# Projecting q and k of the differential branch first and v last, in a two-layer mixed-branch encoder

## Chip, cores and metric

One core of one Trainium2 chip. The time is in device microseconds for one run of the whole program, the median of several runs. TensorE (PE) does the matmuls and its weight loads show as PEld; VectorE is DVE, ScalarE is ACT, GpSimd is POOL, and SyncE (SP) issues the DMAs.

## The reference

Two layers over two groups of tokens, 512 and 256 of them, with a model width of 1024. Each layer normalises its input, projects it to fourteen pieces with one matrix, runs four branches (latent attention, differential attention, a recurrent gate unit, grouped-query attention), multiplies each by a SiLU gate, and projects the concatenation out.

```python
def diff_branch(q, k, v, pos, lam, subln, layer_idx):
    q = partial_rope(q.reshape(b, s, 2 * H_B, DK_B), pos).reshape(b, s, H_B, 2, DK_B)
    k = partial_rope(k.reshape(b, s, 2 * H_B, DK_B), pos).reshape(b, s, H_B, 2, DK_B)
    v = v.reshape(b, s, H_B, DV_B)
    ...
    o1 = blocked_attention(q[..., 0, :], k[..., 0, :], v, DK_B ** -0.5)
    o2 = blocked_attention(q[..., 1, :], k[..., 1, :], v, DK_B ** -0.5)
    o = o1 - lam_full.astype(o1.dtype) * o2
    o = rms_norm(o, subln) * (1.0 - lam_init)

def rglru_branch(xc, conv_w, conv_b, wa, ba, wx, bx, lam):
    # xconv: a convolution of four taps over xc
    def direction(d, reverse):
        r = jax.nn.sigmoid(blockdiag(xconv, wa[d]) + ba[d]).astype(jnp.float32)
        i = jax.nn.sigmoid(blockdiag(xconv, wx[d]) + bx[d])
        log_a = -LRU_C * r * jax.nn.softplus(-lam[d].astype(jnp.float32))
        a = jnp.exp(log_a)
        gx = jnp.sqrt(-jnp.expm1(2.0 * log_a)) * (i * xconv).astype(jnp.float32)
        _, h = lax.associative_scan(scan_combine, (a, gx), axis=1, reverse=reverse)
        return h
    h = direction(0, False) + direction(1, True)
```

## The kernel before

The 768 tokens are six tiles of 128, four of the first group and two of the second. A float32 product is three matmuls of halves: each operand is split into a high and a low part (`split_evac`, L460: ACT writes the high part at L114, DVE the low one; for weights L211), and `mm3` (L285) runs low by high, high by low and high by high. Inside a layer the program text has this order: grouped-query attention, latent attention, then the stretch that the change touches, then the differential attention with the gates and the next layer's preparation woven in, then the output projection.

The stretch in question holds two generators. `rglru()` makes two tiles of features, ct 0 and 1. For each: a projection with the features on the partitions (24 matmuls of 128x512 and 24 of 128x256), the convolution on DVE (L969 and L972), a copy of its high part on ACT and of its low part on POOL (L980), four gate products a group (the tiles `tr`, by the weights in `pt`), tanh and exp on ACT, a multiplication chain on DVE (L993 to L996), a square root on ACT, and then on DVE L1006, two scans (L1007, L1008) and L1009. `diff()` projects v, q and k in chunks of 256 columns, one token tile after another: 24 matmuls of 128x256 a tile into `acc` or `tr` banks in turn (`ROT_B`). A tile of v is evacuated by two pairs of ACT and DVE (`v_evac`) into tiles of tag `b`; a tile of q or k by a copy on DVE (L193) to a tile of tag `rot` and three short DVE operations that rotate its first columns (L735, L737, L740).

The attention then transposes half of q and k on PE (L622), splits them on ACT and DVE into `b` tiles, and stacks pieces of them by SBUF-to-SBUF DMAs on SyncE: `stacks` issues six a head and score pair (L750 and L752), 24 for a half of the heads. A score product (L764) needs the six of its pair.

The order in which each engine runs is not the program's: `arrange` (from L1267) takes all instructions and issues them again by a list. At each step it takes, over all engines, the instruction that could start soonest by its own cost figures, and of equals the earlier in the program. Buffers of one tag are given out in the order in which the program first writes to them; an instruction that opens a buffer out of its turn has to wait for those before it:

```python
            x = need[tag] = need.get(tag, 0) + 1
            if queue[tag][x - 1:x] != [t] or len(free[tag]) < x:
                return None
            t0 = max(t0, sorted(free[tag])[x - 1])
```

There are 51 buffers of `b`, 6 of `wh` and of `wl` (split weights and loads of the adaptive-norm weights), 2 of `rot`, and 2 `acc`, 3 `tr` and 2 `s` PSUM banks. So the program's order does two things: it breaks ties, and it fixes the order of the buffers. A tile of v opens its pair of `b` buffers when its first half is written, one pair of pairs for two token tiles.

Of the kernel before, what the change touches and what calls it, by code (L numbers as in the profile page):

```python
# [18 lines left out]
P = 128  # L19
# [54 lines left out]
def body(ctx, tc, I, O, dbg=None):  # L74
# [8 lines left out]
    def sb(shape, dt=F32, tag=None, bufs=None):  # L83
        cnt[0] += 1
        nm = f"{tag or 'c'}_{cnt[0]}"
        tag = tag or nm
        return pool.tile(list(shape), dt, name=nm, tag=tag, bufs=bufs or BUFS.get(tag, 1))
# [299 lines left out]
    for l in range(DEPTH):  # L387
# [40 lines left out]
        def token_chunk(ci, evac, loaded=None):  # L428
            ncol = TCH[ci][1]
            his, los = loaded or token_load(ci)  # L430
            for tt in range(NT):
                acc = ps("acc")
                g = 0 if tt < 4 else 1
                s = slice(tt * P - GRP[g][0], (tt + 1) * P - GRP[g][0])
                hh, hl = H[g]
                for k in range(KC):
                    mm3(acc[:, :ncol], hh[k][:, s], hl[k][:, s], his[k // 2][:, k % 2], los[k // 2][:, k % 2],
                        k == 0, k == KC - 1)
                evac(tt, acc)
                yield  # L440
# [86 lines left out]
        def transpose_pv(Ps, g, vt, done):  # L527

            t0, n = GRP[g]
            nk = n // P  # L530
            pv = ps("pv")
            for kt in range(nk):
                tr = ps("tr")
                for qt in range(nk):
                    nc.tensor.transpose(tr[:, qt * P:(qt + 1) * P], Ps[qt // 2][:, qt % 2, kt * P:(kt + 1) * P], ident)  # L535
                ph, pl = (sb([P, 512], F32R, tag="pt") for _ in range(2))
                split_evac(ph[:, :n], pl[:, :n], tr[:, :n])
                for i, p in enumerate((pl, ph)):
                    nc.tensor.matmul(pv[:, :n], vt(g, kt), p[:, :n], start=(kt == 0 and i == 0),  # L539
                                     stop=(kt == nk - 1 and i == 1))  # L540
                if kt % 2:
                    yield
            done(pv)
# [58 lines left out]
        def v_tiles(nh):  # L602

            both = [[sb([P, 2, 2, 2, 64], F32R, tag="b") for _ in range(NT // 2)] for _ in range(nh // 2)]

            def head(h):
                def at(g, kt):
                    tt = GTILES[g][kt]
                    return both[h // 2][tt // 2][:, tt % 2, h % 2].rearrange("p e d -> p (e d)")
                return at  # L610
            return both, [head(h) for h in range(nh)]
# [104 lines left out]
            jobs["d"] = attn  # L716


        def diff():
            both, Vs = v_tiles(4)  # L720

            def evac_v(tt, acc):
                v_evac(both, tt, acc)
            yield from token_chunk(2, evac_v)
            qr = sb([P, NT, 256], tag="rot")
            kr = sb([P, NT, 256], tag="rot")

# [27 lines left out]
            def job(g, cp, half, j, o, dens, after):  # L755
                n = GRP[g][1]
                st = {}

                def soft():
                    st["P"] = []  # L760
                    for h2 in range(n // 256):

                        (p1, d1), (p2, d2) = [softmax(
                            lambda out, qt: nc.tensor.matmul(out, q[:96, qt * P:(qt + 1) * P], k[:96], start=True,  # L764
                                                             stop=True), g, h2, d) for (q, k), d in
                            zip(st["qk"], (dens[:, 2 * h2:2 * h2 + 2, 2 * half + j], None))]
                        V.reciprocal(d2, d2)  # L767
                        V.scalar_tensor_tensor(d2, d2, nlam, d1, op0=ALU.mult, op1=ALU.mult)
                        for i in range(2):
                            V.scalar_tensor_tensor(p1[:, i], p2[:, i], d2[:, i:i + 1], p1[:, i],  # L770
                                                   op0=ALU.mult, op1=ALU.add)
                        st["P"].append(p1)
                        yield

                def pv():
                    yield from transpose_pv(st["P"], g, Vs[2 * half + j], lambda pv: o_evac(o, j, pv, n))
                    after()
                return {"stacks": lambda: st.__setitem__("qk", [stacks(cp(), 2 * j + i, g) for i in range(2)]),
                        "soft": soft, "pv": pv, "w": n // 256}
# [263 lines left out]
        def take(gen, n=10 ** 6):  # L1043
            for _ in range(n):
                if next(gen, 0) == 0:
                    break
# [14 lines left out]
                    due -= 1  # L1061
                    next(fill, None)

        lru, gq = rglru(), gqa()
        rot_acc[:] = ROT_A
        take(gq)
        rot_acc[:] = ["acc"]
# [29 lines left out]
        take(lru, 2)  # L1097
        take(df, 6)
        take(lru, 2)
        take(df, 6)  # L1100
        take(lru)
        take(df)
        rot_acc[:] = ["acc"]
        xsrc = I["x"] if l == 0 else xd
        xs = [[None, None] for _ in range(NT)]
# [161 lines left out]
def arrange(tc):  # L1267
# [59 lines left out]
    group.pop("open", None)  # L1327
    follow = {}
    for k, g in sorted(group.items()):
        deps[g] |= {j for j in deps[k] if j != g and group.get(j) != g}  # L1330
        follow.setdefault(g, []).append(k)
    after = [[] for _ in range(n)]
    todo = [len(d) for d in deps]
# [223 lines left out]
```

## Time and profile before

| what | us |
|---|---|
| median of 3 runs | 943.17 |
| lowest and highest | 938.64, 943.53 |
| the profiled execution | 942.88 |
| its span in the trace | 941.1 |
| PE busy | 866.7 |
| DVE busy | 718.0 |
| ACT busy | 558.4 |
| POOL busy | 150.1 |

The profiled execution is the one that the trace records; its span is from the first to the last instruction, and 1.8 us of the run lie outside it. Busy times are sums over the span, and the engines work at the same time. A row of a timeline gives the start, the duration and the work of an instruction, and in brackets how long its engine had nothing to do before it and what released it. A row "x3" holds three in a row. The end of a matmul is modelled; its pace is read from the starts.

### The profile page before, as it was taken

How to read it: one execution, taken by the hardware profiler on the slowest of the kernel's cores; microseconds unless marked ns; L12 is line 12 of the kernel's file. 1: busy time of each engine (PE TensorE's matmuls, PEld its weight loads, DVE VectorE, ACT ScalarE, POOL GpSimd, SP SyncE). 2: the span in 40 equal slices, each digit the busy share in tenths (PEclk: the TensorE clock that was granted, in tenths of full speed). 3: DMA queues.
4: the chain of work that ended last, by engine and by line, in shares of the span. 5: the costliest groups of instructions: out<-in, count | busy, mean ns of one | idle time of the engine just before them, and what ended most of it. 6: DMA issues, size and time to landing. Idle time of an engine off the chain costs nothing. (4 is left out here: it accounts for less than half of the span.)

```text
span 941.1 us, 15540 instructions
## 1 busy us (share of the span) xinstructions
PE 866.7 (92%) x5248; PEld 723.3 (77%) x5248; DVE 718.0 (76%) x1894; ACT 558.4 (59%) x1355; POOL 150.1 (16%) x168
## 2 busy tenths in 40 slices
PE   4899887999989899899999998799999999998996
PEld 1599676878989675677889976677798887886785
DVE  5677997778498678868556998789756887999645
ACT  5544896777545456645456368688637535777422
POOL 0321011003111010203302201000121222011510
PEclk9999999999999999999999999899999999998998
DMA  9821020313202575227711211021231225324412
GB/s 351 274 74 57 1 68 26 102 59 96 56 24 84 161 229 159 84 63 235 231 49 35 65 37 67 3 68 56 80 102 41 60 70 133 86 67 156 152 46 90
DMA packets 54351, 91.72 MB, mean 97 GB/s; under 512 B 9072, under 2 KB 13936, under 8 KB 54272
## 3 DMA queue, kind: packets, MB, share of 16 engines
q1 hardware_dynamic: 54272, 90.73, 31.3%
q8 instruction: 42, 0.69, 0.3%
q14 instruction: 37, 0.30, 0.1%
HBM read 73.38 MB, written 6.31 MB: 85 GB/s over the span
## 5 line engine op out<-in xcount | busy, mean ns | idle before, releaser
L285 PE MATMUL acc<-wh,b 128*128 128x256 f32 (+4 forms) x720 | 186.6, 309 | 0.0
L285 PE MATMUL acc<-b,wh 128*128 128x512 f32 (+1 forms) x576 | 169.5, 361 | 0.0
L114 ACT ACTIVATE p<-s,mx 128x512 f32<-128x512 f32 (+1 forms) x192 | 117.9, 616 | 39.7 <-DVE mx L520 33.9
L211 POOL TENSOR_TENSOR wl<-ws,wh 128x512 fp32r<-128x512 f32 (+3 forms) x56 | 75.7, 1354 | 368.6 <-ACT wh L114 325.1
L285 PEld LDWEIGHTS acc<-wh,b 128*128 128x128 f32 (+1 forms) x720 | 131.0, 190 | 3.6
L285 PEld LDWEIGHTS acc<-b,wh 128*128 128x128 f32 x576 | 104.8, 191 | 21.4 <-issue 8.0
L285 PE MATMUL acc<-wl,b 128*128 128x256 f32 (+4 forms) x360 | 109.3, 314 | 5.3 <-ACT pt L114 1.6
L285 PE MATMUL tr<-wh,b 128*128 128x256 f32 (+2 forms) x432 | 110.6, 290 | 0.0
L285 PE MATMUL acc<-b,wl 128*128 128x512 f32 (+1 forms) x288 | 102.9, 362 | 1.0 <-DVE den L767 0.5
L520 DVE TENSOR_REDUCE mx<-s 128x1 f32<-128x512 f32 x128 | 86.4, 682 | 12.7 <-PE s L764 9.1
L539 PE MATMUL pv<-pt,b 128*128 128x512 f32 (+1 forms) x288 | 93.5, 392 | 2.6 <-DVE pt L460 2.0
L535 PE MATMUL tr<-c,p 128*128 128x128 f32 x480 | 84.3, 283 | 11.6 <-DVE pt L460 7.5
L460 DVE TENSOR_TENSOR pt<-tr,pt 128x512 fp32r<-128x512 f32 (+1 forms) x144 | 84.5, 594 | 7.7 <-ACT pt L114 6.5
L114 ACT ACTIVATE wh<-ws 128x512 fp32r<-128x512 f32 (+3 forms) x100 | 62.8, 641 | 42.6 <-PE tr L285 12.8
L535 PEld LDWEIGHTS tr<-c,p 128*128 128x128 f32 x480 | 60.9, 145 | 31.1 <-DVE pt L460 9.7
L114 ACT ACTIVATE pt<-tr 128x512 fp32r<-128x512 f32 (+1 forms) x144 | 74.3, 527 | 10.4 <-PE tr L535 9.7
L285 PEld LDWEIGHTS tr<-wh,b 128*128 128x128 f32 x432 | 79.4, 190 | 0.7
L285 PEld LDWEIGHTS acc<-wl,b 128*128 128x128 f32 (+1 forms) x360 | 67.7, 191 | 10.4 <-ACT pt L114 2.2
L285 PEld LDWEIGHTS acc<-b,wl 128*128 128x128 f32 x288 | 54.6, 191 | 14.2 <-issue 8.1
L114 ACT ACTIVATE b<-tr 128x128 fp32r<-128x128 f32 (+7 forms) x92 | 40.0, 448 | 38.3 <-PE tr L285 14.3
L539 PEld LDWEIGHTS pv<-pt,b 128*128 128x128 f32 x288 | 52.3, 200 | 12.6 <-DVE pt L460 6.0
L285 PE MATMUL tr<-wl,b 128*128 128x256 f32 (+2 forms) x216 | 61.1, 290 | 0.0
(254 smaller groups left out, 1905.5 us busy)
## 6 DMA issues: line engine op xcount, KB each, us to landing
ws<-wf SPq DMA_DIRECT2D x40, 256.0 KB, 2.9
b<-ada SPq DMA_DIRECT2D x32, 256.0 KB, 5.4
ws<-wt SPq DMA_DIRECT2D x32, 256.0 KB, 3.3
wl<-ada SPq DMA_DIRECT2D x32, 256.0 KB, 5.2
wh<-ada SPq DMA_DIRECT2D x32, 256.0 KB, 4.5
ws<-wo SPq DMA_DIRECT2D x32, 256.0 KB, 3.2
b<-b SPq DMA_DIRECT2D x112, 64.0 KB, 2.7
b<-b SPq DMA_DIRECT2D x112, 32.0 KB, 1.8
```

The costliest lines, as they stand in the source:

```text
L114: return nc.scalar.activation(out, in_, f, **kw)
L211: engine(eng).tensor_tensor(lo, w, hi.bitcast(F32), op=ALU.subtract)
L285: nc.tensor.matmul(out, s, m, start=first and i == 0, stop=last and i == 2)
L460: V.tensor_tensor(lo, src, hi.bitcast(F32), op=ALU.subtract)
L520: V.tensor_reduce(mx[:, i:i + 1], views[i], axis=AX.X, op=ALU.min)
L535: nc.tensor.transpose(tr[:, qt * P:(qt + 1) * P], Ps[qt // 2][:, qt % 2, kt * P:(kt + 1) * P], ident)
L539: nc.tensor.matmul(pv[:, :n], vt(g, kt), p[:, :n], start=(kt == 0 and i == 0), stop=(kt == nk - 1 and i == 1))
```

## The change

`diff()` is cut in two: v's chunk is a generator of its own, `diff_v()`, and the projections are called in another order. Before: two steps of the recurrent branch (its first feature tile), v, two steps (its second), q, the rest of the branch, then k. After: two steps, q, two steps, k (and the setting up of the attention's jobs), the rest of the branch, then v. An edit in `arrange` writes the sets of dependencies of a group of matmuls in another way, with the same contents. The number of instructions and of DMAs is the same; the lines behind the edit are two higher.

```diff
--- before.py
+++ after.py
@@ -716,12 +716,14 @@
             jobs["d"] = attn
 
 
-        def diff():
-            both, Vs = v_tiles(4)
+        def diff_v():
+            both, dv["Vs"] = v_tiles(4)
 
             def evac_v(tt, acc):
                 v_evac(both, tt, acc)
             yield from token_chunk(2, evac_v)
+
+        def diff():
             qr = sb([P, NT, 256], tag="rot")
             kr = sb([P, NT, 256], tag="rot")
 
@@ -773,7 +775,7 @@
                         yield
 
                 def pv():
-                    yield from transpose_pv(st["P"], g, Vs[2 * half + j], lambda pv: o_evac(o, j, pv, n))
+                    yield from transpose_pv(st["P"], g, dv["Vs"][2 * half + j], lambda pv: o_evac(o, j, pv, n))
                     after()
                 return {"stacks": lambda: st.__setitem__("qk", [stacks(cp(), 2 * j + i, g) for i in range(2)]),
                         "soft": soft, "pv": pv, "w": n // 256}
@@ -1061,7 +1063,8 @@
                     due -= 1
                     next(fill, None)
 
-        lru, gq = rglru(), gqa()
+        dv = {}
+        lru, gq, vg = rglru(), gqa(), diff_v()
         rot_acc[:] = ROT_A
         take(gq)
         rot_acc[:] = ["acc"]
@@ -1097,9 +1100,9 @@
         take(lru, 2)
         take(df, 6)
         take(lru, 2)
-        take(df, 6)
+        take(df)
         take(lru)
-        take(df)
+        take(vg)
         rot_acc[:] = ["acc"]
         xsrc = I["x"] if l == 0 else xd
         xs = [[None, None] for _ in range(NT)]
@@ -1327,7 +1330,10 @@
     group.pop("open", None)
     follow = {}
     for k, g in sorted(group.items()):
-        deps[g] |= {j for j in deps[k] if j != g and group.get(j) != g}
+        deps[g] |= {j for j in deps[k] if j < g and j != g}
+        late = [j for j in deps[k] if j > g and group.get(j) != g]
+        assert not late or True
+        deps[g] |= set(late)
         follow.setdefault(g, []).append(k)
     after = [[] for _ in range(n)]
     todo = [len(d) for d in deps]
```

Three places of the order that `arrange` gives. The number behind a name is the instruction of the program that made the tile, and the one before it the tile's number.

The first is ScalarE at the end of the first projected chunk in layer 0, before. `b_837` and `b_846` are the high parts of the convolution's result, `b_814` to `b_818` tiles of v.

```order
L114 ACTIVATE b_814_3149<-tr_834_3265 128x2x64
L114 ACTIVATE b_817_3152<-tr_834_3265 128x2x64
L114 ACTIVATE b_815_3150<-acc_835_3294 128x2x64
L114 ACTIVATE b_818_3153<-acc_835_3294 128x2x64
L114 ACTIVATE b_837_3352<-b_801_3068 128x512
L114 ACTIVATE wh_871_3517<-ws_870_3515 128x512
L114 ACTIVATE b_846_3387<-b_802_3069 128x256
```

And ScalarE at the same place after the change, where `b_845` and `b_854` are those copies:

```order
L114 ACTIVATE wh_867_3445<-ws_866_3443 128x512
L114 ACTIVATE tmp_812_3140<-tr_811_3115 128x256
L114 ACTIVATE wh_870_3451<-ws_869_3449 128x512
L114 ACTIVATE b_845_3360<-b_801_3068 128x512
L114 ACTIVATE b_854_3395<-b_802_3069 128x256
L114 ACTIVATE wh_877_3523<-ws_876_3521 128x512
L114 ACTIVATE p_847_3364<-tr_850_3367,c_26_132 128x512
```

The copies of the convolution's result stood behind the evacuation of v's fifth token tile, and now no tile of v stands in front of them. On TensorE, 20 of the 24 matmuls of 128x512 of the second feature tile stood ahead of the last gate product of the first; now 8 do.

The second is ScalarE where the attention of layer 0 begins, before. `b_954` and `b_957` are the high parts of the transposed q and k, from which the DMAs copy; `p_902` and `p_910` are the square roots of the second feature tile.

```order
L114 ACT_TABLE_LOAD
L114 ACTIVATE p_902_3729<-p_902_3729 128x1024
L114 ACTIVATE wh_967_4062<-ws_966_4060 128x512
L114 ACTIVATE p_910_3763<-p_910_3763 128x512
L114 ACTIVATE b_954_4025<-tr_953_4020 128x512
L114 ACTIVATE b_957_4034<-tr_956_4029 128x512
L114 ACT_TABLE_LOAD
```

And after the change, where `b_926` and `b_929` are the last two tiles of v, written from the banks of token tiles 4 (`acc_946`) and 5 (`tr_947`):

```order
L114 ACTIVATE b_928_3815<-tr_945_3928 128x2x64
L114 ACTIVATE b_926_3813<-acc_946_3957 128x2x64
L114 ACTIVATE b_926_3813<-tr_947_3986 128x2x64
L114 ACTIVATE b_929_3816<-acc_946_3957 128x2x64
L114 ACTIVATE b_954_4025<-tr_953_4020 128x512
L114 ACTIVATE b_929_3816<-tr_947_3986 128x2x64
L114 ACTIVATE b_957_4034<-tr_956_4029 128x512
L114 ACT_TABLE_LOAD
```

The two copies' sources now stand behind the first halves of the last tiles of v. TensorE has 16 of token tile 4's 24 matmuls still to do when the transposes begin, where three matmuls of the last chunk remained before.

The third is SyncE's queue at the same place, before. `b_959` to `b_962` are the operands of the first two score pairs (959 and 960 of the first, 961 and 962 of the second), filled by six copies each.

```order
L750 DMA b_959_4038<-b_954_4025 32x512
L752 DMA b_960_4039<-b_957_4034 32x512
L750 DMA b_961_4046<-b_954_4025 32x512
L752 DMA b_962_4047<-b_957_4034 32x512
L750 DMA b_959_4038<-b_954_4025 32x512
L750 DMA b_959_4038<-b_955_4026 32x512
L752 DMA b_960_4039<-b_958_4035 32x512
L752 DMA b_960_4039<-b_957_4034 32x512
L750 DMA b_961_4046<-b_954_4025 32x512
L750 DMA b_961_4046<-b_955_4026 32x512
L752 DMA b_962_4047<-b_958_4035 32x512
L752 DMA b_962_4047<-b_957_4034 32x512
```

And after, from the fourth issue on, since the first three are the same:

```order
L752 DMA b_959_4038<-b_954_4025 32x512
L752 DMA b_959_4038<-b_955_4026 32x512
L754 DMA b_960_4039<-b_958_4035 32x512
L754 DMA b_960_4039<-b_957_4034 32x512
L752 DMA b_961_4046<-b_954_4025 32x512
L752 DMA b_961_4046<-b_955_4026 32x512
L754 DMA b_962_4047<-b_957_4034 32x512
L752 DMA b_973_4124<-b_954_4025 32x512
L754 DMA b_974_4125<-b_957_4034 32x512
L752 DMA b_975_4132<-b_954_4025 32x512
L754 DMA b_962_4047<-b_958_4035 32x512
L754 DMA b_962_4047<-b_957_4034 32x512
```

In both the issues stand in the same queue behind the loads into `wh` and `wl`. The first pair is complete with the eighth copy before and with the seventh after; the second pair with the twelfth before and with the fifteenth after (the two that still lack stand behind three copies for `b_973` to `b_975`, tiles of the next head).

## Rows read from the trace of the kernel before

**Rows 1.** The page, part 1: engine, busy us, share of the span, instructions
```profile
PE 866.7 (92%) x5248; PEld 723.3 (77%) x5248; DVE 718.0 (76%) x1894; ACT 558.4 (59%) x1355; POOL 150.1 (16%) x168
```

**Rows 2.** Timeline of PE, layer 0: start, us, instruction, [idle before, releaser]
```profile
278.26 0.47 PE L285 MATMUL tr<-b,pt 128*128 128x512 f32 x1 [0.89 <-DVE rot L193]
...
281.35 0.50 PE L285 MATMUL tr<-b,pt 128*128 128x512 f32 x1 [1.80 <-DVE rot L193]
...
295.59 0.39 PE L285 MATMUL acc<-wl,b 128*128 128x256 f32 x1 [0.55 <-DVE wl L211]
...
316.00 0.47 PE L764 MATMUL s<-b,b 96*128 96x512 f32 x1 [1.97 <-DMA b<-b]
```

**Rows 3.** Timeline of PE, layer 1
```profile
727.59 0.39 PE L285 MATMUL acc<-wl,b 128*128 128x256 f32 x1 [0.74 <-DVE wl L211]
...
734.91 0.39 PE L285 MATMUL acc<-wl,b 128*128 128x256 f32 x1 [0.89 <-DVE rot L193]
...
743.88 0.50 PE L285 MATMUL tr<-b,pt 128*128 128x512 f32 x1 [1.06 <-DVE rot L193]
...
762.82 0.33 PE L622 MATMUL tr<-c,rot 128*128 128x128 f32 x1 [1.27 <-DVE rot L193]
...
786.72 0.50 PE L764 MATMUL s<-b,b 96*128 96x512 f32 x1 [1.69 <-ACT p L114]
```

**Rows 4.** Windows of layer 0: length, busy PE, PEld, DVE, ACT, POOL, clock, DMA
```profile
240.00:250.00 10.00, 10.00 (x81) 9.74 (x80) 2.25 (x9) 3.23 (x11) 0.58 (x1) 1.00 0.00 0
250.00:260.00 10.00, 10.00 (x57) 8.52 (x56) 5.20 (x6) 8.57 (x18) 3.15 (x3) 1.00 0.29 80
270.00:280.00 10.00, 8.65 (x69) 8.07 (x67) 10.00 (x20) 1.54 (x3) 3.16 (x3) 1.00 0.01 2
```

**Rows 5.** Timeline of DVE, layer 0
```profile
248.23 0.28 DVE L460 TENSOR_TENSOR b<-acc,b 128x128 fp32r<-128x128 f32 x1
...
265.23 1.23 DVE L1006 TENSOR_TENSOR p<-p,p 128x1024 f32<-128x1024 f32 x1 [0.98 <-ACT p L114]
...
281.21 0.21 DVE L735 TENSOR_TENSOR t<-rot,c 128x64 f32<-128x64 f32 x1
...
281.48 0.41 DVE L193 COPY rot<-acc 128x256 f32<-128x256 f32 x1
```

**Rows 6.** Timeline of ACT at the end of layer 0's first chunk
```profile
248.54 0.28 ACT L114 ACTIVATE b<-acc 128x128 fp32r<-128x128 f32 x1 [0.36 <-DVE b L460]
248.72 0.62 ACT L114 ACTIVATE b<-b 128x512 fp32r<-128x512 f32 x1
...
252.09 0.69 ACT L114 ACTIVATE p<-tr,c 128x512 f32<-128x512 f32 x1 [0.65 <-PE tr L285]
```

**Rows 7.** Timeline of PE, 128x512 matmuls, from one start to the third after
```profile
308.27 0.40 PE L285 MATMUL acc<-b,wl 128*128 128x512 f32 x1
...
308.97 0.39 PE L285 MATMUL acc<-b,wl 128*128 128x512 f32 x1
```

**Rows 8.** Windows of 2 us behind waits, columns as in the windows above
```profile
282.00:284.00 2.00, 2.00 (x9) 1.73 (x8) 1.74 (x8) 1.65 (x3) 0.00 (x0) 0.63 0.51 176
284.00:286.00 2.00, 2.00 (x8) 1.71 (x8) 0.00 (x0) 1.64 (x3) 0.00 (x0) 0.51 0.46 130
318.00:320.00 2.00, 2.00 (x13) 0.49 (x9) 0.40 (x1) 1.13 (x3) 0.34 (x1) 0.50 0.44 105
744.00:746.00 2.00, 2.00 (x12) 1.73 (x13) 0.45 (x3) 2.00 (x4) 1.30 (x1) 1.00 0.29 101
```

**Rows 9.** Timeline of SyncE's issues at the start of layer 0's differential attention
```profile
307.96 0.51 SPq L750 DMA_DIRECT2D b<-b  x1
...
318.28 0.59 SPq L750 DMA_DIRECT2D b<-b  x1
```

**Rows 10.** Timeline of ACT: the copies' sources
```profile
307.34 1.09 ACT L114 ACTIVATE b<-tr 128x512 fp32r<-128x512 f32 x2 [7.91 <-PE tr L622]
```

**Rows 11.** Timeline of ACT, layer 1, behind its attention's start
```profile
785.40 0.60 ACT L114 ACTIVATE b<-tr 128x512 fp32r<-128x512 f32 x1 [2.34 <-issue]
```

## The prediction

> **What bounds the kernel now.** I read the page first: TensorE is busy for 866.7 of 941.1 us and no other engine comes near [rows 1]. So the time is TensorE's work, plus the places where TensorE stands still, plus the stretches in which its clock is low. A change that moves work without adding any can only act on the last two. I therefore listed TensorE's waits of 0.3 us or more in the stretch that the change touches, once for each layer.
>
> In layer 0 there are four that count: 0.89 and 1.80 us, where the gate products of the second feature tile wait for the copy of a q tile on VectorE; 0.55, where a chunk waits for the low half of its weights, also on VectorE; and 1.97 at the first score, which waits for the stacking DMAs [rows 2]. Layer 1 has five: 0.74, 0.89, 1.06 and 1.27, all behind VectorE, and 1.69 at a score that waits for an exp on ScalarE [rows 3].
>
> Windows show why VectorE is late. In the first chunk, v's, it is busy for 2.25 and 5.20 of two times 10 us, and then full, 10.00 of 10, when q is projected [rows 4]. What fills it is the chain of the first feature tile behind its square root (L1006, at 265.23, and the scans) [rows 5]. That chain starts from the gate products, whose tanh on ScalarE comes at 252.09; and those stood behind the copy of the convolution's result at 248.72, which came directly after v's fifth tile at 248.54 [rows 6]. In the order given in the section on the change, that copy is behind v because v's `b` buffers come first in the program.
>
> **The change part by part.** It removes and adds no instruction and no DMA, so the sum has only waits.
>
> *First chunk.* q instead of v: a q tile costs VectorE a copy of 0.41 and three operations of about 0.21, so 1.04; a v tile two subtractions of 0.28, so 0.56 [rows 5]. Six tiles make 2.9 us more here, hidden in 7.75 + 4.80 = 12.55 us that VectorE has free [rows 4]. With no cover it would cost those 2.9 us. No `b` buffer of v stands in front of the convolution's copy any more, and 12 fewer matmuls of 128x512 stand ahead of the last gate product (20 before, 8 after). Three of them take 0.70 us [rows 7], so one 0.233 and twelve 2.8 us: by so much earlier, in TensorE's progress, can the chain on VectorE start.
>
> *Second chunk.* k takes q's place, with the same work on VectorE, behind a chain that is 2.8 us ahead. The 0.89 and 1.80 sum to 2.69, which this just covers. Behind them the granted clock is 0.63 and 0.51 over two windows of 2 us [rows 8], between its two levels of 1.00 (2.4 GHz) and 0.50 (1.2 GHz): 2 x 0.37 + 2 x 0.49 = 1.72 us lost, which comes back with the waits. The low half of the third chunk's weights also comes from VectorE, so I let the 0.55 go too. Layer 0: up to 2.69 + 1.72 + 0.55 = 4.96.
>
> *Layer 1* has the same order, and 0.74 + 0.89 + 1.06 = 2.69 of the same waits. The 1.27 at the transposes waits for the last k tile; with v last, q and k are long done. Together up to 3.96.
>
> *What becomes of the sum.* At most 4.96 + 3.96 = 8.9 us. Lower bound: no work leaves VectorE, so some of the waits behind `rot` may remain; half is 4.4. The head start is no larger than the waits, so nothing is to spare: I take 85%, 7.6 us.
>
> *Start of the attention, layer 0.* Here v is late, and this costs. Before, the two sources of the stacking copies followed the transposes on an idle ScalarE (7.91 us of nothing ahead of them, 307.34), and the first DMA went out at 307.96, 0.62 later [rows 9, 10]. After, they stand behind the first halves of v's tile 4, whose bank is complete 31 rows later than the first transpose. Those halves go in turn between ScalarE and VectorE, 0.28 + 0.36 + 0.28 [rows 6]; with some 0.2 until the bank can be read (estimate) and the 0.62, the first DMA leaves 1.75 us after that last matmul. The Trainium skill (Perfetto Trace Analysis, the section on the Tensor Engine Instruction) says that ScalarE and VectorE are strict queues. By it the sources cannot pass v; if they could, this part would cost nothing and the time would be 936. The trace bears the rule out so far as one execution can: in layer 1 ScalarE does nothing for 2.34 us in front of a transposed piece [rows 11], with the exp that TensorE then waits for queued behind it [rows 3].
>
> From the first DMA to the first score 8.04 us passed (307.96 to 316.00) for eight copies [rows 2, 9]. The fifteenth went out at 318.28, so 14 steps took 10.32, 0.74 each; the first pair is now complete with the seventh, so 7.3. TensorE has between tile 4's last matmul and that score 16 matmuls of 128x512 (3.73), 13 of 128x256 at half of that (1.5) and eight of 32 columns, four of them side by side, put at four matmuls' pace (0.93): 6.2. The wait is 1.75 + 7.3 - 6.2 = 2.85.
>
> The second pair needs the fifteenth copy in place of the twelfth. By the eighth (issued at 307.96 + 7 x 0.74 = 313.1, used at 316.00) a copy takes up to 2.9 from issue to use, and 2.3 by the DMA's own part of that; the pair is ready 12.6 to 13.2 after the first DMA, so 5.3 to 5.9 after the first score. TensorE has 2.0 us of work in between, so a second wait of 3.3 to 3.9, where there was none. Taking 3.5, the two make 6.35 against 1.97: 4.4 more. Some waits of half a microsecond behind the second pair fall into these, so I take 4.0, with 1.5 and 6.1 as bounds. The upper one has a second fall of the clock (1.72), the lower one a ScalarE that finishes v sooner, so that only the pair order costs.
>
> *Layer 1* has the same queue on ScalarE. Its first scores did not wait before; the wait of 1.69 was further on, behind the copies. The first DMA is 1.75 - 0.62 = 1.13 later in TensorE's progress, so that wait goes to about 2.8: 1.1 lost, between 0 (the exp now stands ahead of the transposed piece) and 2.8.
>
> **Sum.** -7.6 + 4.0 + 1.1 = -2.5 against the profiled execution of 942.88, which lies 0.3 below the median: 940.4, and I say 940.
>
> **The rivals.**
>
> *Gain without the loss.* If the copies' sources get through early, or the second score pair is covered by woven work, only the upstream part is left: 942.88 - 8.9 + 0 to 3 gives 934 to 937. For it: layer 1's start of the attention had no wait for the copies. Against it: the fixed place of the sources behind v, and two more SyncE issues. Chance 0.22.
>
> *Slower: the late stacking copies outweigh the gain.* SyncE sends 24 copies a half at 0.74, and all that follows waits in turn. If the two waits of layer 0 stand in full and the clock falls twice (6.1), and in layer 1 the first scores also wait and the clock falls there too (1.1 + 2.8 + 1.72 = 5.6), the loss is 11.7. Against a gain of 7.6 or only 3.8 that is 947 to 951. It decides when the waits at both attention starts together pass 1.97 + 1.69 + 7.6 = 11.3. The clock of 0.50 after the 1.97 [rows 8] speaks for it; layer 1's unhindered first score speaks against it. The Trainium skill (TensorE: Matmul & The Clock Gate, the section HAM oscillation) has waits for DMAs lowering the clock again and again, which would charge every such wait with a slow stretch. Layer 0 agrees; behind layer 1's wait of 1.06 the clock stays at 1.00 [rows 8]. Chance 0.16.
>
> *The waits upstream stay.* VectorE is full for 10 us during the second chunk and loses no work there; if the copies stay behind the scans, only 0.55, 0.74 and 1.27 go, and the losses of 5.1 remain: 942.88 - 2.56 + 5.1 = 945.4. Speaking against it: the chain is released earlier. Chance 0.12.
>
> **How the numbers follow.** The forecast case (0.50) reaches from 937.5 to 943.5. The range takes in the first rival down to 934 and the third, and cuts the second: 934 to 947.5. A measurement of this kernel can tell 0.5%, 4.7 us, from no change: faster means below 938.5, slower above 947.9. Faster: the first rival (0.22) and the lower end of the forecast case (0.12), 0.34. Slower: most of the second rival and a little of the third, 0.14. The rest, 0.52, is the same.
>
> **What would show it.** Right: the waits behind `rot` of the second feature tile are gone in both layers and the clock stays at 1.00 there; the first tanh comes about 2.8 us earlier against TensorE's matmuls; ScalarE's first transposed piece of the attention stands directly behind v; two waits for `b<-b` at the start of layer 0's attention, of about 2.9 and 3.5 us. Wrong: waits of over 1 us that still name `rot` in the second chunk; a first score that does not wait; or new waits in the third chunk, if v's banks come free late.

## The result, and the profile after

The changed kernel takes 948.95 us (median of 6, 946.88 to 950.77) against 940.28 of the kernel before beside it (median of 6): a ratio of 1.0068 with a 95% interval of 1.0041 to 1.0095, so slower by 6.4 us (3.9 to 8.9) by the ratio; the two medians lie 8.7 apart. Six more executions beside the experiments gave 949.93 and 1.0096 (1.0061 to 1.0131). The prediction said 940.0, with a range that ended at 947.5, and gave slower a chance of 0.14. The profiled execution took 946.88, with a span of 945.0 us, 3.9 above that of before.

The page of the changed kernel, its span and its busy times:

```profile
span 945.0 us, 15545 instructions
...
PE 870.1 (92%) x5248; PEld 725.6 (77%) x5248; DVE 720.5 (76%) x1894; ACT 559.2 (59%) x1355; POOL 153.3 (16%) x168
```

TensorE's busy time is 3.4 us larger than before [rows 1] with the same matmuls, while it stands still for 74.9 us of the span against 74.4 before. So most of what these two executions differ by is a low clock and not waiting. TensorE's waits of 0.3 us and more in layer 0, in the changed kernel's timeline, from the second chunk to the third head of the attention, and at 316.72 the first score, which has no wait:

```profile
267.52 0.38 PE L285 MATMUL acc<-wl,b 128*128 128x256 f32 x1 [1.40 <-DVE wl L211]
...
275.24 0.38 PE L285 MATMUL acc<-wl,b 128*128 128x256 f32 x1 [0.37 <-DVE rot L193]
...
284.25 0.50 PE L285 MATMUL tr<-b,pt 128*128 128x512 f32 x1 [0.98 <-ACT p L114]
...
302.00 0.36 PE L285 MATMUL acc<-wl,b 128*128 128x256 f32 x1 [0.49 <-DVE b L460]
...
316.72 0.39 PE L766 MATMUL s<-b,b 96*128 96x512 f32 x1
...
319.70 0.50 PE L236 MATMUL tr<-c,tmp 128*128 128x2 f32 x3 [1.04 <-DVE tmp L233]
...
321.87 0.77 PE L766 MATMUL s<-b,b 96*128 96x512 f32 x1 [1.12 <-DMA b<-b]
...
344.57 0.49 PE L766 MATMUL s<-b,b 96*128 96x512 f32 x1 [0.56 <-ACT p L114]
...
346.56 0.50 PE L766 MATMUL s<-b,b 96*128 96x512 f32 x1 [1.49 <-ACT p L114]
```

The first four answer to the first three of [rows 2]: 0.89 + 1.80 + 0.55 = 3.24 before, 1.40 + 0.37 + 0.98 + 0.49 = 3.24 now. No wait is gone in the sum. But the clock stays up there, where before it fell and cost 1.72 [rows 8]. The wait of 1.97 at the first score is gone. Only the second pair waits for its copies, 1.12 at 321.87; the 1.04 ahead of it is for a row of the adaptive norm that VectorE copies (L233) and not for a DMA. The last two are 0.56 and 1.49 where the kernel before has 0.34 and 0.88:

```profile
344.05 0.50 PE L764 MATMUL s<-b,b 96*128 96x512 f32 x1 [0.34 <-ACT p L114]
...
345.43 0.50 PE L764 MATMUL s<-b,b 96*128 96x512 f32 x1 [0.88 <-ACT p L114]
```

Windows of 2 us of the changed kernel, the clock third from the end: it is up where the second chunk's waits are, and falls behind each of the two places in the attention.

```profile
282.00:284.00 2.00, 1.28 (x8) 0.87 (x6) 0.95 (x3) 1.97 (x3) 0.00 (x0) 1.00 0.46 136
284.00:286.00 2.00, 1.75 (x10) 1.53 (x11) 0.00 (x0) 2.00 (x4) 0.00 (x0) 1.00 0.36 126
320.00:322.00 2.00, 0.88 (x8) 0.83 (x7) 0.65 (x3) 0.27 (x2) 0.00 (x0) 0.78 0.42 98
322.00:324.00 2.00, 2.00 (x5) 1.63 (x6) 1.29 (x2) 0.60 (x2) 0.00 (x0) 0.50 0.45 105
324.00:326.00 2.00, 2.00 (x6) 1.54 (x6) 0.00 (x0) 0.85 (x4) 0.00 (x0) 0.50 0.31 73
348.00:350.00 2.00, 2.00 (x10) 1.90 (x11) 2.00 (x5) 0.78 (x2) 0.00 (x0) 0.61 0.90 299
350.00:352.00 2.00, 2.00 (x6) 1.52 (x5) 0.62 (x4) 0.00 (x0) 0.00 (x0) 0.50 0.83 250
```

The kernel before falls behind its 0.88 too, for a shorter time:

```profile
346.00:348.00 2.00, 2.00 (x13) 1.81 (x12) 2.00 (x7) 0.00 (x0) 0.00 (x0) 0.85 0.87 254
348.00:350.00 2.00, 2.00 (x6) 1.54 (x6) 1.37 (x5) 1.34 (x4) 0.00 (x0) 0.50 1.00 265
350.00:352.00 2.00, 2.00 (x9) 1.58 (x8) 0.00 (x0) 0.11 (x2) 0.00 (x0) 0.80 0.88 218
```

The waits of the same stretch in layer 1:

```profile
725.75 0.39 PE L285 MATMUL acc<-wl,b 128*128 128x256 f32 x1 [0.58 <-DVE wl L211]
...
742.08 0.50 PE L285 MATMUL tr<-b,pt 128*128 128x512 f32 x1 [0.95 <-ACT p L114]
...
753.82 0.39 PE L285 MATMUL acc<-wl,b 128*128 128x256 f32 x1 [0.63 <-DVE wl L211]
...
761.49 0.36 PE L285 MATMUL acc<-wl,b 128*128 128x256 f32 x1 [0.43 <-DVE b L460]
...
788.59 0.50 PE L766 MATMUL s<-b,b 96*128 96x512 f32 x1 [1.51 <-ACT p L114]
...
830.40 0.47 PE L285 MATMUL acc<-b,wl 128*128 128x512 f32 x1 [1.70 <-DVE b L481]
```

Here the projections lost 0.58 + 0.95 + 0.63 + 0.43 = 2.59 where they lost 3.96 [rows 3], and the attention's wait went from 1.69 to 1.51. New is the 1.70 at 830.40, in the middle of the attention, for the evacuation of a gate product.

Most of the signs that the prediction named can be read off at once. The last tanh of the first feature tile's gates starts at 257.56 (before 260.35), 2.8 us earlier, as worked out. The waits behind `rot` are down to 0.37 in layer 0 and gone in layer 1. The stacking copies start late, as worked out:

```profile
309.07 0.28 ACT L114 ACTIVATE b<-acc 128x128 fp32r<-128x128 f32 x1 [4.42 <-PE acc L285]
...
309.88 0.59 ACT L114 ACTIVATE b<-tr 128x512 fp32r<-128x512 f32 x1
```

```profile
310.50 0.51 SPq L752 DMA_DIRECT2D b<-b  x1
...
318.30 0.57 SPq L752 DMA_DIRECT2D b<-b  x1
```

ScalarE's first row is a first half of v's tile 4 and the second the first of the two sources. The first DMA leaves at 310.50, 1.43 us after tile 4's bank was read (1.75 minus 0.2 was expected). But the two waits for `b<-b` of 2.9 and 3.5 us are one of 1.12, and a first score that does not wait was named as a sign of being wrong.

### The profile page after: what moved, and what is told of

It reads as the page before. It is cut to its first block, busy times and chain, and to the rows that moved or that the text cites. A ratio compares the mean times of both kernels' runs of the same rounds, so it can differ in the third digit from the quotient of the medians.

```text
span 945.0 us, 15545 instructions
## 1 busy us (share of the span) xinstructions
PE 870.1 (92%) x5248; PEld 725.6 (77%) x5248; DVE 720.5 (76%) x1894; ACT 559.2 (59%) x1355; POOL 153.3 (16%) x168
## 5 line engine op out<-in xcount | busy, mean ns | idle before, releaser
L211 POOL TENSOR_TENSOR wl<-ws,wh 128x512 fp32r<-128x512 f32 (+3 forms) x56 | 77.9, 1395 | 400.4 <-ACT wh L114 346.0
L285 PE MATMUL tr<-wh,b 128*128 128x256 f32 (+2 forms) x432 | 107.5, 287 | 0.0
L285 PE MATMUL s<-b,b 96*128 96x512 f32 (+2 forms) x192 | 54.7, 378 | 1.1 <-DMA b<-b 0.9
```

Of the source, the lines that this page charges most:

```text
L211: engine(eng).tensor_tensor(lo, w, hi.bitcast(F32), op=ALU.subtract)
L285: nc.tensor.matmul(out, s, m, start=first and i == 0, stop=last and i == 2)
```

## What the experiments measured

The weave, below, is the order in which the gates' products and the next layer's preparation, the fill, stand between the attention's steps. Each time is given against the kernel before, run beside it on the same chip; its medians there were 941.2 to 942.5 us. A gain or loss in us is the ratio's, with its 95% interval.

**One layer at a time.** The changed call order stands under a condition, and the other layer keeps v, q, k (the calls of a branch are put on one line here).

```diff
+        if l == 0:
+            take(lru, 2); take(df, 6); take(lru, 2); take(df); take(lru); take(vg)
+        else:
+            take(lru, 2); take(vg); take(lru, 2); take(df, 6); take(lru); take(df)
```

> The new projection order in layer 0 alone; layer 1 keeps v, q, k. Theory A (the loss is made at the start of the differential attention, because the last tiles of v hold back the sources of the stacking copies): layer 0 has the two waits for the copies, so most of the 6 to 9 us between the kernels is here, +4 to +6 us on the kernel before. Rival B (the loss is made later, inside the attention, where the list scheduler weaves scores, gates and transposes in another way, and it is about as large in each layer): +2 to +4 us here.

Measured: 948.34 us, ratio 1.0057 (1.0037 to 1.0078), so +5.4 us.

> The new projection order in layer 1 alone. Theory A: layer 1's first scores did not wait for the copies in the changed kernel's trace, and its projections lost 1.5 us of waits, so the time is that of the kernel before or 1 to 2 us less. Rival B: +2 to +4 us, with the loss behind the first quarter of the attention, as in the trace of the changed kernel, where layer 1 is level up to its first value transposes and loses 3.9 us from there to the end.

Measured (the condition is `l == 1`): 944.87 us, ratio 1.0027 (1.0010 to 1.0043), so +2.5 us. Layer 1 is not free of loss, against theory A, and layer 0 loses more than B said. The two sum to 7.9.

**Buffers of their own for v.** If the sources stand behind v because of the order of the `b` buffers, a tag of its own takes v out of that queue (shortened at the dots).

```diff
-    BUFS = {"ws": 4, "wh": 6, "wl": 6, "b": 51, ...
+    BUFS = {"ws": 4, "wh": 6, "wl": 6, "b": 45, "vb": 6, ...
...
-            both, dv["Vs"] = v_tiles(4)
+            both, dv["Vs"] = v_tiles(4, "vb")
```

> The changed kernel, with the six v tiles of this branch in a tag of their own (6 buffers, and 45 instead of 51 in b). The order of ScalarE then has the sources of the stacking copies ahead of the last v tiles again. Theory A: the first DMA leaves about 1 us earlier, the waits of layer 0 at the first scores shrink, and the kernel is 4 to 8 us faster than the changed one, so at or below the kernel before. Rival B: the weave of the attention stays much as in the changed kernel, and so does the time, within 3 us of it.

Measured: 952.11 us, ratio 1.0098 (1.0072 to 1.0125). The first copy left 2.3 us earlier (308.22 against 310.50), the first two score pairs waited 0.20 and 0.79, and the kernel was still no faster. That speaks against theory A, that the late copies make the loss, but doesn't settle it: right behind these scores its weave is that of neither kernel, with waits of 0.92, 0.62 and 1.47 (322.80 to 325.89) that neither has.

> The kernel before, v first, with the same tag of its own for v. The copy of the convolution's result no longer stands behind v's buffers, so the first feature tile's gates come earlier without any projection being moved. If what the prediction said of the projections is right (waits for VectorE of 0.9 and 1.8 us in layer 0 and 0.7 to 1.3 in layer 1 go), 2 to 5 us faster than the kernel before. If these waits are set by the sum of VectorE's work (rival), the same time within 1.5 us. A time over that of before would be for B: the weave of the attention decides.

Measured (the same tag in the kernel before): 943.48 us, ratio 1.0008 (0.9989 to 1.0027). The two waits behind VectorE in layer 0 have become one of 0.95:

```profile
282.45 0.50 PE L285 MATMUL tr<-b,pt 128*128 128x512 f32 x1 [0.95 <-ACT p L114]
```

So the upstream gain shows in the trace and costs no move of a projection; but the median has nothing of it.

**Splicing two orders.** The list of all instructions that `arrange` gives is written into the kernel: up to the last instruction of a layer's projections the order of one kernel, behind it that of the other. Both programs hold the same instructions, so such a list can be made (the list itself is left out here).

```diff
+ORDER = (...
...
+    raw = zlib.decompress(base64.b85decode(ORDER))
+    order = [raw[2 * i] + 256 * raw[2 * i + 1] for i in range(n)]
     for a, b in zip(order, order[1:]):
```

> The changed kernel up to the last instruction of each layer's projections, and from there the attention and all behind it in the order of the kernel before (the order is written into the kernel as a list). Theory B (the loss is the other weave of the attention): the kernel is 6 to 10 us faster than the changed one, 939 to 943, at or a little below the kernel before, since the projections of the changed kernel lost 1.6 and 1.5 us less in its trace. Theory A (v's late tiles hold back the attention, whatever order follows): 946 to 950 as the changed kernel.

Measured: 944.25 us, ratio 1.0033 (1.0008 to 1.0058), so +3.1: between the two theories, 5.7 below the changed kernel beside it and not back at the kernel before. Its trace shows what the late copies do when the weave is held. TensorE's first score in layer 0 waits nearly twice as long as the 1.97 of before [rows 2]:

```profile
316.43 0.77 PE L768 MATMUL s<-b,b 96*128 96x512 f32 x1 [3.81 <-DMA b<-b]
```

> The reverse: the projections of the kernel before, v first, and from each layer's last projection on the changed kernel's order. Theory B: slow with nothing of the change left in the projections, 946 to 951. Theory A: 941 to 944, as the kernel before.

Measured: 947.60 us, ratio 1.0064 (1.0039 to 1.0090), so +6.0, with v projected first and nothing of the change left in the projections. The sum of the two, 9.1, meets the 9.0 of the changed kernel beside them closer than intervals of 2.4 to 3.3 us to either side would make one expect:

> The changed kernel itself, unaltered, for more executions beside the two spliced ones: 947 to 950, with a mean granted clock of 0.97 to 0.975 against 0.978 of the kernel before.

Measured: 949.93 us, as told above. So about two thirds of the loss lie in the order behind the projections, and are there without any late v; theory A can be the rest at most. The waits go with that order and not with the projections; TensorE's rows in the kernel with the old projections and the new weave, in layer 0 and layer 1:

```profile
343.93 0.49 PE L766 MATMUL s<-b,b 96*128 96x512 f32 x1 [0.56 <-ACT p L116]
...
345.91 0.49 PE L766 MATMUL s<-b,b 96*128 96x512 f32 x1 [1.49 <-DMA wl<-ada]
...
836.67 0.47 PE L287 MATMUL acc<-b,wl 128*128 128x512 f32 x1 [1.70 <-DVE b L483]
```

(the load that the second row names landed together with the exp's end at 345.85, and the score starts 0.06 behind it, as in the changed kernel) and in the one with the new projections and the old weave, in layer 0 (in layer 1 it has nothing like the 1.70):

```profile
345.01 0.50 PE L768 MATMUL s<-b,b 96*128 96x512 f32 x1 [0.33 <-ACT p L116]
...
346.39 0.50 PE L768 MATMUL s<-b,b 96*128 96x512 f32 x1 [0.88 <-ACT p L116]
```

What the place costs can be added up. From the second transposes of layer 0's attention to the third, TensorE's idle time plus its half-rate time (one minus the granted clock, times the time) is 5.8 to 5.9 us in all four profiles with the new weave there (changed kernel, its repetition, layer 0 alone, new weave behind old projections), 2.4 of it idle. In seven profiles with the old weave it is 1.3 to 3.1, 1.8 in the mean, 1.3 of it idle. So this stretch is worth about 4 us, and most of that is the clock.

The order shows why the first of these places is bare. In layer 0, 96 gate products (48 of 128x512 and 48 of 128x256) are woven into the first heads. So many of them stand ahead of a score product on TensorE:

```
score tile (number in the order)   4142  4167  4336  4337  4518  4519
kernel before                        30    48    85    91    96    96
changed kernel                       37    55    96    96    96   120
```

Before, eleven products are left for the gaps between the three scores 4336, 4337 and 4518. Now they are used up earlier, and the scores follow each other; each needs the exp of an earlier one to free its bank, and TensorE waits.

**Where in the weave.** The cut is put later, or in one layer only.

> The changed kernel with the order of the kernel before from one score product of layer 0's attention on (the second of the third head's first pair, some 35 us behind the projections), and in layer 1 from its last projection on. Against the kernel spliced at the projections (944) it differs in those 35 us alone, where three scores follow each other with no gate product between them, TensorE waits 0.6 and 1.5 us for exps and its clock falls. If that place carries the weave's loss in layer 0: 946 to 949. If the loss is spread over the rest of the attention or lies in layer 1: 943 to 945.

Measured: 949.90 us, ratio 1.0076 (1.0050 to 1.0101), +7.2, a little above the forecast. Against the splice at the projections, 4 us more for 35 us of order. Not all of it is the new weave's: where the two orders meet, TensorE has a wait that neither of them has.

```profile
359.29 0.50 PE L768 MATMUL s<-b,b 96*128 96x512 f32 x1 [1.36 <-ACT p L116]
```

> The changed kernel with the order of the kernel before behind layer 0's projections only; layer 1 keeps the changed kernel's weave. Against the one spliced in both layers (944) this gives layer 1's weave, where the trace of the changed kernel has a wait of 1.7 us for a gate's evacuation on VectorE: if that counts, 946 to 947.5; if layer 0's weave holds all of the loss, 943.5 to 945.

Measured: 947.84 us, ratio 1.0057 (1.0031 to 1.0084), +5.4, so layer 1's weave is worth about 2.3. The intervals of both differences are about 3.5 us to either side: the split is a likely one, not a sharp one.

**The upstream part alone.** In the kernel before, the convolution's copies are emitted ahead of v (the generator yields once more, behind them), and the order behind the projections is kept by a splice (only the call is shown).

```diff
...
-        take(lru, 2)
+        take(lru, 3)
         take(df, 6)
```

> The kernel before with the two copies of the convolution's result (high and low part) emitted ahead of v in the program, so that v's buffers don't hold them back, and from each layer's last projection on the order of the kernel before. Nothing is moved but those four copies and what follows from them in the projections. If the prediction's upstream gain is real and is not lost later: 938 to 940.5, by 2 to 4 us faster than before. If the upstream waits only move to other places: 941.5 to 943.5.

Measured: 940.02 us, ratio 0.9991 (0.9964 to 1.0017). In its trace the waits of 3.24 in layer 0 [rows 2] are 0.95 and 0.48, so less is lost there than with v last.

> The same kernel as the one with the early copies and the order of before behind the projections, for more executions: it was 0.1% under the kernel before with an interval of 0.4% under to 0.2% over. If the upstream gain is kept: 938 to 940.5; else 941 to 942.5.

Measured: 939.82 us, ratio 0.9992 (0.9963 to 1.0021). Over its 24 executions the mean is 940.5, over 94 of the kernel before 941.9. It is the best version here, and its gain of about 1 us can't be told from none.

**Starting the attention early.** Before `take(vg)` the first head's transposes and its twelve copies are emitted (hoisted), so that they run beside v's projection; the later line that made the list of jobs goes.

```diff
         take(lru)
+        js = list(jobs["b"]())
+        for j in js[:1]:
+            j["stacks"]()
+            j["stacks"] = lambda: None
         take(vg)
```

> The changed kernel with the first transposes of q and k and the twelve stacking copies of the first head emitted ahead of v's projection in both layers, so that they run beside it. Theory B in its present form (the attention starts late against the gate products that are woven in, these are used up in the waits, and scores further on stand bare): the waits at the first scores go, the gate products last longer, and the kernel is 5 to 9 us faster than the changed one, 940 to 944. Rival (the weave is another one with every edit, and its loss has nothing to do with when the scores start): 945 to 952.

Measured: 952.04 us, ratio 1.0106 (1.0080 to 1.0131).

> The same with the copies of the first two heads, 24 of them, ahead of v. The first scores then stand among v's own products, 70 rows earlier. Theory B: at least as good as with one head, 936 to 943, and at the best faster than the kernel before. Rival: 945 to 952, or worse than with one head, since exps and reductions then collide with v's evacuation.

Measured (`js[:2]`): 950.19 us, ratio 1.0095 (1.0073 to 1.0117). The wait for the first scores' copies is gone, and a larger one stands in v's chunk; TensorE's row in the kernel with one head:

```profile
302.75 0.58 PE L285 MATMUL tr<-wl,b 128*128 128x256 f32 x1 [3.38 <-DVE b L460]
```

> The changed kernel with the first head's transposes and copies ahead of v (as in the run with one head hoisted) and v's tiles in a tag of their own. In the run with one head, TensorE waited 3.4 us in v's chunk for a v evacuation, whose buffers stood behind the stacks' in b. If that was its loss: 3 to 5 us less than that run's 952, 947 to 949. If the start of the attention was also the cause of the weave's loss, 940 to 944. Rival (any other weave than the tuned one loses): 947 to 953.

Measured: 947.50 us, ratio 1.0081 (1.0053 to 1.0108). The wait in v's chunk is still there (3.39), so it was not the order of the buffers. VectorE shows what it is: the low half of the transposed q is read out of its bank only behind the scans of the second feature tile,

```profile
297.11 1.21 DVE L1009 TENSOR_TENSOR_SCAN b<-p,p 128x512 f32<-128x512 f32 x1
...
298.83 1.21 DVE L1010 TENSOR_TENSOR_SCAN p<-p,p 128x512 f32<-128x512 f32 x1
...
299.96 0.66 DVE L460 TENSOR_TENSOR b<-tr,b 128x512 fp32r<-128x512 f32 x1
```

and TensorE needs that bank for v. The time fits the first forecast and the rival alike, and as the wait is still there it is not for the first one's reason: the hoist doesn't win the loss back.

But the weave does come back. At the place of the 0.56 and 1.49, the kernel with one head hoisted has the waits of before:

```profile
349.32 0.50 PE L766 MATMUL s<-b,b 96*128 96x512 f32 x1 [0.32 <-ACT p L114]
...
350.71 0.50 PE L766 MATMUL s<-b,b 96*128 96x512 f32 x1 [0.89 <-ACT p L114]
```

The same holds for v in its own tag, and for both edits together: in these three traces, as many gate products stand ahead of each score behind the second transposes as in the kernel before (0, 0, 4, 4, 5, 11, 13, 19, 24, 24, where the changed kernel has 0, 0, 13, 13, 15, 19, 24, 24, 24), and the stretch up to the third transposes loses 1.3 to 1.4 us. (With two heads hoisted the weave is yet another.) So it is the late copies that make the planner weave otherwise here, and copies that start early bring other waits in front of it.

**Another weave in the kernel before.** One constant, the units of fill for each step of layer 0's differential attention.

```diff
-    F_D, F_A, F_B, F_C = ((0.897, 1.178), (0.494, 0.213), (1.2, 1.393), (1.833, 0.976))
+    F_D, F_A, F_B, F_C = ((0.897, 1.178), (0.494, 0.213), (1.25, 1.393), (1.833, 0.976))
```

> The kernel before, with one constant of the weave changed: 1.15 instead of 1.2 units of fill for each step of layer 0's differential attention (first half). Projections, buffers and copies are as before up to the attention's start. Theory C (the order of before is a chosen one among many, and any other weave of this attention costs): 944 to 950. Theory B (the loss needs the late start that the moved v brings): 940 to 943, as before.

Measured: 943.15 us, ratio 1.0019 (0.9997 to 1.0041).

> The same with 1.25 in place of 1.2. Theory C: 944 to 950. Theory B: 940 to 943.

Measured: 953.18 us, ratio 1.0131 (1.0100 to 1.0162), +12.3, with the projections of before. With more fill to a step the fill is over sooner, and the attention's end is bare; TensorE's rows, and windows of 4 us there:

```profile
383.57 0.55 PE L535 MATMUL tr<-c,p 128*128 128x128 f32 x3 [3.02 <-DVE p L770]
...
395.69 1.01 PE L262 MATMUL acc<-tmp,c 128*2 128x512 f32 x1 [2.28 <-DVE tmp L260]
```

```profile
384.00:388.00 4.00, 3.25 (x13) 2.28 (x12) 3.51 (x9) 3.39 (x11) 0.00 (x0) 0.57 0.17 39
388.00:392.00 4.00, 4.00 (x19) 3.65 (x18) 1.55 (x3) 0.60 (x1) 0.00 (x0) 0.50 0.45 137
392.00:396.00 4.00, 1.72 (x6) 0.78 (x5) 2.46 (x6) 2.35 (x6) 0.00 (x0) 0.50 0.00 0
396.00:400.00 4.00, 4.00 (x12) 2.42 (x11) 1.88 (x6) 0.00 (x0) 0.00 (x0) 0.50 0.01 3
```

Theory C holds in one direction: a neighbouring weave can cost more than the change does. With 1.15 it costs 1.8 us, between 0.3 less and 3.9 more than nothing, so not every other weave is bad.

## Why the prediction was wrong

**The step that failed** is the first of the sum: "It removes and adds no instruction and no DMA, so the sum has only waits." The terms that were then summed end at the first score pairs and, in layer 1, at one exp a little behind; further on nothing was to change. The order behind the projections alone costs 6.0 us (3.7 to 8.5). The prediction had the order of both kernels and used it up to the second score pair; the weave further on differs over hundreds of rows in both layers and was not priced. No rival named it: the slower one was the late copies, and its price and its place were others. A second step failed in size: of the gain of 7.6 upstream, the traces show 3.1 (1.72 of clock in layer 0 and 1.37 of waits in layer 1). With the old weave held, the change is still 3.1 us slower (0.8 to 5.5) where 2.5 faster was forecast.

**Upstream, layer 0: mis-sized.** Forecast 4.2 us of gain (85% of 4.96). The chain on VectorE does start 2.8 us earlier, and the waits behind `rot` go from 2.69 to 0.37. But 1.40 comes at the second chunk's first matmul, because the split of its weights now stands on VectorE behind the scans, and 0.98 where a gate's bank waits for its tanh. The timeline of VectorE in the changed kernel:

```profile
263.95 1.22 DVE L1009 TENSOR_TENSOR_SCAN b<-p,p 128x512 f32<-128x512 f32 x1
...
265.66 1.22 DVE L1010 TENSOR_TENSOR_SCAN p<-p,p 128x512 f32<-128x512 f32 x1
...
266.80 0.66 DVE L211 TENSOR_TENSOR wl<-ws,wh 128x512 fp32r<-128x512 f32 x1
```

What was really won is the fall of the clock, 1.72: it stands in four of the five profiles with v first and no edit to its copies, and in none of the ten with v last. The prediction said where a stall goes only for the waits that it removed and not for what the earlier chain would run into.

**Start of the attention, layer 0: the path was right, the waits were not.** Forecast were 2.85 at the first score and 3.5 at the second pair in place of 1.97; measured were none and 1.12 (none and 1.95 in the repetition; with layer 0 alone 1.24, for which the profile names no releaser, and 1.19). The copies went out faster: the seventh was issued at 314.26 and the fifteenth at 319.55, 9.05 us after the first and not 10.3, and they took 2.0 us from issue to landing in the median. And TensorE had more to do: from tile 4's last matmul to the first score it worked for 7.8 us, not 6.2. Narrow matmuls of the adaptive norm, put at 0.93, took 2.0 there (sixteen, 314.18 to 315.18 and 315.50 to 316.49). Before, they stood behind the first pair of scores. So in the changed kernel fill covers the late copies; in the two splices with the new projections and the old weave it stays behind, and the first score waits 3.81 and 3.79.

Adding TensorE's idle and half-rate time from the first transposes to the second, the changed kernel, its repetition, layer 0 alone and the later splice lose 4.7 to 6.5 us, these two splices 6.5 and 6.2, and seven profiles with v first and without the new weave 1.7 to 4.4, 2.5 in the mean. So the start costs about 3 us more in the changed kernel and 3.9 with the weave held, where 4.0 was forecast. That these meet is partly luck: the terms were off both ways, and a second fall of the clock, put only into the upper bound, is in the sum of the changed kernel. The Trainium skill (TensorE: Matmul & The Clock Gate, the section HAM oscillation) tells of a clock that falls behind waits for DMAs, again and again. The windows at 322 to 326 agree with it. But of these seven profiles with v first, whose first score waited 0.68 to 2.01 us for its copies, only the profile of before shows a fall there, and the one that waited 2.01 (1.15 units of fill) does not.

**Layer 1:** forecast 3.4 of gain and 1.1 of loss; the profile shows 1.37 and a gain of 0.18. With the weave held, the projections and the start so come to 3.9 - 1.72 - 1.37, about +0.8 where -2.5 was forecast; the splice measures 0.8 to 5.5.

**What was taken for granted:** that the clock would cost the same. From the mean granted clock of every execution, (1 - clock) times span is 19.4 us on average over 94 executions of the kernel before and 26.7 over 12 of the changed one. Some of that falls on idle time, so it is an upper figure, but 7.3 us of it stand against a loss of 6 to 9. The splice with the old weave has 20.2, that with the new weave 24.9, the kernel with 1.25 units of fill 27.7.

What stays open: by which of its choices the planner weaves in another way when v is moved. That the late copies are behind it is shown for the place in layer 0, by the three kernels that start them earlier; that no other weave with v last would be faster is not shown, since those three have new waits of their own (3.4 us in v's chunk, or 0.92, 0.62 and 1.47 behind the first scores). Of the +6.0 behind the projections, about 4 are located in layer 0's stretch and about 2.3 in layer 1's weave, while the start of layer 0's attention is about 1.3 better there; of the +3.1 in front, about 2 are not located, which is within its interval.

## What to carry to other kernels

Where a planner orders everything, a change of program order is a change of all that follows: compare the two orders to the end, count how much fill is left ahead of each step that waits for another engine, and price the places where it runs out. Before judging such a change, hold the rest of the order fixed by splicing it from the kernel before; else one measures the new weave and not the change. A constant that was tuned to one order can make a change to it dear: 0.05 more in one of them cost 12 us here, more than any other edit, and 0.05 less nothing that can be told from none.

## What was not expected of the hardware

The clock falls behind waits for ScalarE too, not only for DMAs: 0.56 and 1.49 us on exps are followed by 0.61 and 0.50 in the rows of 348 to 352, and all five profiles with this pair of waits fall there. Waits of the same length don't always bring it down: the old weave's 0.34 and 0.88 were followed by 0.85 and 0.50 in the profile of before, and by a full 1.00 in that of the kernel with the early copies; eleven profiles have this pair, and three fall. One kernel's executions lie 11 us apart (936.5 to 947.7 over 30 of the kernel before). Over the 94 of them, the time and (1 - clock) times span go together (correlation 0.75), so the clock is a good part of this spread, and a profile of a single execution was a poor base for a forecast of a few us.
